# Layer 0 of a two-layer decoder trunk: another matmul form for the 16 recurrence projections, and another order of gates, outputs and heads

## The chip, the cores and the metric

The kernel runs on one core of a Trainium2 chip. The metric is device time in microseconds (us) of one execution; three runs of the kernel before gave a median of 2206.34 us (2206.28 to 2206.48). The engines that matter: TensorE (PE in the profile, its weight loads PEld), VectorE (DVE), ScalarE (ACT), and SyncE (SP), which issues the weight transfers. Each engine works through its own queue in the order in which the program was laid out, and waits on semaphores where an operand or a buffer is not ready.

## The reference, cut to what matters

The trunk has a batch of one, 256 tokens and a width of 2048. Layer 0 projects the normalised input into a recurrence (RG-LRU, 1024 wide, with a gated output) and into eight HGRN2 heads, and maps both through one output projection; a squared-ReLU MLP follows. Layer 1 is attention with an MLP. The change touches only layer 0's mixer:

```
proj = h @ w_in
x_lru, y_lru, q_h, f_h, v_h, g_h = jnp.split(proj, list(IN_SPLITS), axis=-1)
lru = rg_lru(causal_depthwise_conv(x_lru, conv_w, conv_b), w_a, b_a, w_i, b_i, lam)
lru = lru * jax.nn.gelu(y_lru.astype(F32), approximate=True)
hg = hgrn2(q_h, f_h, v_h, g_h, lower_bound, g_norm)
mixed = jnp.concatenate([lru, hg], axis=-1).astype(h.dtype)
return mixed @ w_out
```

Inside `rg_lru`, the two gates `r` and `i` are block-diagonal products (four blocks of 256) of the convolved `x_lru`, each through a sigmoid; `a` is an exponential of `r`, and a scan over the 256 tokens gives the recurrence.

## The kernel before

**Precision.** Every float32 matmul is made of three: each operand is split into a high part (rounded to fp32r) and a low part (the rest), and high·high, high·low and low·high are added in PSUM. Weights come in tiles of 128x2048; `Weights.split` makes `hi` (a ScalarE cast, line 104) and `lo` (a VectorE subtraction, line 105), in two halves of 128x1024 in this stage. `hi`, `lo` and `raw` have three buffers each, so a tile's split waits until the tile three before it is used up.

**Two forms of one projection.** A projection (`project`) makes a 128x256 block of features by tokens from 16 blocks of the input. The activations stand in `bufa` as 16 blocks of 512 columns: 256 of the high part, 256 of the low part. `direct` (lines 210 to 216) issues per block three matmuls of 256 columns (hi by high, hi by low, lo by high), all into the same 256 columns of PSUM. `cross` (lines 204 to 208) issues per block one matmul of 512 columns (hi by high and low at once, into two halves of a PSUM bank), and, after all 16 of them, 16 matmuls of 256 columns for lo by high. The halves of the bank must then be added: `scaled` (line 408) copies the second half to SBUF on ScalarE (line 414), adds the first half on VectorE (line 415) and multiplies by the norm's scale (line 416). After `direct`, one VectorE multiplication does (line 411). The MLP's up-projections use `cross`; `HA`, `XA` and `YA` (line 218) say which form the heads, the recurrence's inputs and its outputs use.

**The order.** `ORDER` (line 853) lists layer 0's steps; it also sets the order in which weights are fetched. `v` (two steps) makes the values of four heads: 4 weight tiles, matmuls of 512 columns into two PSUM banks, copied out by ScalarE (line 345) into `vg`. That pool has one buffer, so the second `v` can be copied out only when head 3 has used the first. `h` is a head: three projections (q, f, g) and between them a ladder of dependent steps: lines 471 (two small matmuls), 474 (a masked copy, VectorE) and 488 (a multiplication, VectorE), for group sizes 1 to 64, then lines 466 and 495 to 497 and a transpose (line 509). `x` is a recurrence input: one projection, then line 525 on ScalarE, three VectorE steps on line 527 (the convolution), and the split into `bufb` (lines 230 and 231). `g` makes the gates of four x blocks: one weight tile, eight PSUM tiles of six 256-column matmuls each, every one copied out by a ScalarE sigmoid; then tanh, exp and sqrt on ScalarE with table loads between, VectorE steps on lines 545 to 553 and a scan (line 554). `y` is an output: one projection, a GeLU made of a square, a sigmoid and VectorE steps on lines 562 to 565, and the split into `bufb`. `out_project` then multiplies `bufb` by the output weights, in groups 2, 3 (heads), 0, 1 (recurrence).

**What sets the order of the work.** Projection and gate matmuls go through `mm`, which chains them: on PE they stand in the order of the program text. The ladder's matmuls are not in the chain; the framework's scheduler puts them between. `lut` keeps ScalarE's table functions in program order, group by table. There are three PSUM banks for projections and gates (`pmm`); `pl` has two, `pd`, `po` and `pt` one each.

Of the kernel before, what the change touches and what calls it, by code (L numbers as in the profile page):

```python
# [40 lines left out]
def trunk_kernel(ctx, tc, x, xtok, cols, tab, masks, pos, fin, w_in, w_gate, w_out, w_qkv, w_o, w1, w2, out):  # L41
# [28 lines left out]
    def plan2(i, products):  # L70
# [3 lines left out]
        for what, u in PRODUCTS:  # L74
# [3 lines left out]
             "v": (w_in, lambda i: 16 + 16 * i, 4), "h": (w_in, lambda i: 20 + i // 4 * 16 + i % 4 * 3, 3)}  # L78
    for step in ORDER.split():
        src, first, n = where[step[0]]  # L80
# [134 lines left out]
            mm(p, h, mov[:, S:], start=False, stop=False)  # L215
            mm(p, l, mov[:, :S], start=False, stop=last)

    HA, XA, YA = direct, direct, direct

    def folded(p, name="z", bufs=None, home=None):  # L220
        with urgent():
# [346 lines left out]
    vgroups = {}  # L568
    for step in ORDER.split():
        i = int(step[1])  # L570
# [279 lines left out]

PRIO = 150
URGENT = 400
ORDER = "v0 h0 x0 h1 x1 h2 x2 h3 x3 v1 h4 x4 h5 x5 h6 x6 h7 x7 g0 y0 y1 y2 y3 g1 y4 y5 y6 y7"
WARM = 12
LINE = 64
PAIRS = 2
# [107 lines left out]
```

## Time and profile before

| | us |
|---|---|
| median of three runs | 2206.34 |
| profiled execution | 2206.14 |
| its span on the core | 2204.3 |
| PE busy | 2180.6 |
| DVE busy | 1673.1 |
| ACT busy | 1110.0 |

The span is the time from the first to the last instruction of the program in the profile; 1.8 us of the profiled execution lie outside of it. "Busy" for PE counts pipelined matmuls whose ends overlap, so that the price of one matmul is not its duration in a row but the distance from its start to the next one's start. A row of the timeline gives the start (us from the span's start), the time from the first start to the last end of the merged instructions, the engine, the line, the tiles and their shapes, and in brackets the idle time before it with what ended it. Layer 0's mixer takes about the first 336 us; then come the output projection, the MLP and layer 1.

### The profile page before, as it was taken

Reading aid. Unit: us, or ns where it says so; the run is one execution under the profiler, and the core shown is the slowest. Engines: PE = TensorE matmul, PEld = TensorE weight load, DVE = VectorE, ACT = ScalarE, POOL = GpSimd, SP = SyncE. Lnnn points to the kernel's source line nnn. Section 1 sums busy time; section 2 is a strip of 40 time slices with the busy share of each in tenths; the row PEclk is TensorE's granted clock in tenths of the full one; section 3 lists DMA queues with packets and bytes.
Section 4 is the critical chain, followed back from the end, with each engine's and each line's share of the span. In section 5 each row is a group of like instructions: output and inputs, shape, how many; then the busy total and the mean of one; then the engine's idle time right before and its main releaser. Section 6 shows DMA issues by size and latency. Waiting matters only on the chain.

```text
span 2204.3 us, 29702 instructions
## 1 busy us (share of the span) xinstructions
PE 2180.6 (99%) x12004; PEld 1897.7 (86%) x12004; DVE 1673.1 (76%) x2286; ACT 1110.0 (50%) x1364; POOL 15.8 (1%) x23
## 2 busy tenths in 40 slices
PE   9999999999999999999999999999999999999997
PEld 8999998888888888888888888888888888888886
DVE  8767796578878877877967868556797697687787
ACT  6444485545444444544654444454454454455454
POOL 0000000000000000000000000000000000000000
PEclk9999999999999999999999999999999999999999
DMA  8444446555655755755654554655566566566553
GB/s 313 156 168 156 153 154 232 181 198 191 232 199 181 248 194 172 248 208 165 217 195 169 174 188 157 227 191 179 165 214 246 174 205 248 191 191 248 191 191 115
DMA packets 61017, 431.25 MB, mean 196 GB/s; under 512 B 6784, under 2 KB 7552, under 8 KB 9424
## 3 DMA queue, kind: packets, MB, share of 16 engines
q1 hardware_dynamic: 58320, 412.20, 53.2%
q0 software_dynamic: 2560, 17.16, 4.3%
q8 instruction: 94, 1.54, 0.3%
q14 instruction: 43, 0.35, 0.0%
HBM read 427.48 MB, written 2.10 MB: 195 GB/s over the span
## 4 chain that ended last, share of the span: by engine, by line
PE 84%; DVE 9%; ACT 3%; DMA 2%; issue 1%; SPq 0%; ACTq 0%; DVEq 0%
PE p L176 75%; DVE lo L105 5%; PE po L176 5%; DVE a L142 2%; ACT hi L104 2%; DMA a<-in_w 2%; PE pd L176 1%; PE pl L471 1%; DVE xall L650 1%; PE pl L179 0%; PE pl L777 0%; DVE bufa L234 0%; PE po L798 0%; DMA xall<-in_x 0%; PE pd L790 0%
## 5 line engine op out<-in xcount | busy, mean ns | idle before, releaser
L105 DVE TENSOR_TENSOR lo<-raw,hi 128x1024 fp32r<-128x1024 f32 (+2 forms) x486 | 822.1, 1709 | 341.8 <-ACT hi L104 322.2
L104 ACT CAST hi<-raw 128x1024 fp32r<-128x1024 f32 (+2 forms) x486 | 688.2, 1441 | 663.3 <-PE p L176 515.3
L176 PE MATMUL p<-bufa,hi 128*128 128x512 f32 (+1 forms) x3840 | 854.5, 357 | 2.4 <-DVE bufa L234 2.4
L176 PEld LDWEIGHTS p<-bufa,hi 128*128 128x128 f32 x3840 | 672.0, 190 | 95.2 <-DVE bufa L234 3.8
L176 PE MATMUL p<-bufa,lo 128*128 128x256 f32 x3200 | 521.9, 285 | 0.0
L176 PEld LDWEIGHTS p<-bufa,lo 128*128 128x128 f32 x3200 | 452.6, 191 | 12.7
L176 PE MATMUL p<-hi,bufb 128*128 128x512 f32 x1408 | 451.9, 391 | 1.6 <-DVE xall L650 1.6
L176 PEld LDWEIGHTS p<-hi,bufb 128*128 128x128 f32 x1408 | 264.5, 188 | 59.1 <-DVE xall L650 5.0
L176 PE MATMUL p<-lo,bufb 128*128 128x512 f32 x704 | 275.3, 391 | 3.8 <-DVE lo L105 3.8
L104 ACT CAST hi<-a 128x2048 fp32r<-128x2048 f32 x64 | 122.4, 1913 | 161.7 <-PE p L176 81.1
L105 DVE TENSOR_TENSOR lo<-a,hi 128x2048 fp32r<-128x2048 f32 x64 | 146.5, 2289 | 58.4 <-ACT hi L104 58.4
L176 PEld LDWEIGHTS p<-lo,bufb 128*128 128x128 f32 x704 | 132.3, 188 | 33.7 <-DVE lo L105 7.2
L176 PE MATMUL p<-hi,bufa 128*128 128x512 f32 x384 | 123.6, 396 | 0.7 <-ACT hi L104 0.7
L176 PEld LDWEIGHTS p<-hi,bufa 128*128 128x128 f32 x384 | 72.3, 188 | 16.0 <-ACT hi L104 1.6
L176 PE MATMUL pd<-hi,bufb 128*128 128x512 f32 x256 | 84.3, 390 | 0.2 <-DVE xall L650 0.2
L176 PE MATMUL po<-hi,bufb 128*128 128x512 f32 x256 | 84.2, 390 | 0.3 <-DVE xall L650 0.3
L176 PE MATMUL p<-hi,forms 128*128 128x512 f32 x256 | 84.1, 389 | 0.0
L176 PE MATMUL p<-lo,bufa 128*128 128x512 f32 x192 | 76.3, 397 | 1.8 <-DVE lo L105 1.8
L142 DVE TENSOR_TENSOR a<-a,raw 128x2048 f32<-128x2048 f32 x32 | 73.1, 2283 | 0.0
L223 ACT COPY t<-p 128x256 f32<-128x256 f32 x128 | 46.7, 365 | 41.2 <-PE p L176 40.7
L650 DVE SCALAR_TENSOR_TENSOR xall<-p,nm,xall 128x512 f32<-128x512 f32 x64 | 47.7, 746 | 19.3 <-PE p L176 19.2
L230 ACT CAST bufb<-zp 128x256 fp32r<-128x256 f32 x128 | 50.4, 401 | 18.7 <-DVE zp L684 18.7
(239 smaller groups left out, 1803.6 us busy)
## 6 DMA issues: line engine op xcount, KB each, us to landing
raw<-in_w SPq DMA_DIRECT2D x224, 1024.0 KB, 4.8
raw<-in_w_qkv SPq DMA_DIRECT2D x48, 1024.0 KB, 4.8
raw<-in_w_in SPq DMA_DIRECT2D x46, 1024.0 KB, 4.8
raw<-in_w_out SPq DMA_DIRECT2D x16, 1024.0 KB, 4.8
a<-in_w SPq DMA_DIRECT2D x16, 1024.0 KB, 4.8
t<-in_w SPq DMA_DIRECT2D x16, 1024.0 KB, 5.0
t<-in_w POOLq DMA_DIRECT2D x16, 1024.0 KB, 8.0
raw<-in_w_o SPq DMA_DIRECT2D x16, 1024.0 KB, 4.8
```

Source lines behind the costliest of these rows:

```text
L104: A.copy(h, w)
L105: V.tensor_tensor(l, w, h.bitcast(F32), OP.subtract)
L142: V.tensor_tensor(r, r, held[add], OP.add)
L176: chain[:] = [after(T.matmul(*args, **kw), chain)]
L223: A.copy(t, p[:, S:])
L230: A.copy(dst[:, :S], src)
L471: T.matmul(pl[:, j], kq[:, js], halves(qp[:, js], c, True), start=True, stop=True)
L650: V.scalar_tensor_tensor(xres[:, j, at], bank, (r2 if sign > 0 else r2n)[:, j:j + 1], xres[:, j, at], op0=OP.mult, op1=OP.add)
```

## The change

Two lines change. The recurrence's input and output projections go from `direct` to `cross`, and the steps of `ORDER` are rearranged: `g0` (the gates of x blocks 0 to 3) now follows `v1`, the outputs `y0` to `y3` stand one behind each of the heads 4 to 7, and `g1` follows `x7` at once.

```diff
-    HA, XA, YA = direct, direct, direct
+    HA, XA, YA = direct, cross, cross
@@
-ORDER = "v0 h0 x0 h1 x1 h2 x2 h3 x3 v1 h4 x4 h5 x5 h6 x6 h7 x7 g0 y0 y1 y2 y3 g1 y4 y5 y6 y7"
+ORDER = "v0 h0 x0 h1 x1 h2 x2 h3 x3 v1 g0 h4 y0 x4 h5 y1 x5 h6 y2 x6 h7 y3 x7 g1 y4 y5 y6 y7"
```

The form that the 16 projections now use, and what follows it:

```python
def cross(p, w, jobs):
    for blk, mov, first, last in jobs:
        mm(p, w.part(blk * P, P)[0], mov, start=first, stop=False, skip_group_check=True)
    for blk, mov, first, last in jobs:
        mm(p[:, S:], w.part(blk * P, P)[1], mov[:, :S], start=False, stop=last, skip_group_check=True)

def scaled(p, z, acc=None):
...
            t = tmp.tile([P, S], F32, name="t1", bufs=2)
            A.copy(t, p[:, S:])
            V.tensor_tensor(z, p[:, :S], t, OP.add)
            V.tensor_tensor(z, z, rs, OP.mult)
```

The order of the weight transfers follows `ORDER`; their number and sizes stay.

## The prediction

> **What bounds the kernel now.** I read the page's head and its chain of waits first.
>
> ```profile
> span 2204.3 us, 29702 instructions
> PE 2180.6 (99%) x12004; PEld 1897.7 (86%) x12004; DVE 1673.1 (76%) x2286; ACT 1110.0 (50%) x1364; POOL 15.8 (1%) x23
> PE 84%; DVE 9%; ACT 3%; DMA 2%; issue 1%; SPq 0%; ACTq 0%; DVEq 0%
> ```
>
> TensorE fills the span; a stage gets shorter only when its matmuls take less or when PE waits less. The layer's stages by windows (length, then busy time of PE, PEld, DVE and ACT, POOL, granted clock, DMA share, GB/s):
>
> ```profile
> 50.00:164.50 114.50, 114.50 (x883) 110.49 (x882) 83.04 (x201) 49.76 (x89) 0.00 (x0) 1.00 0.48 162
> 164.50:272.10 107.60, 107.53 (x910) 107.34 (x909) 78.67 (x192) 48.45 (x93) 0.00 (x0) 1.00 0.46 157
> 272.10:335.85 63.75, 62.69 (x522) 62.17 (x521) 58.14 (x143) 53.01 (x102) 0.52 (x1) 1.00 0.45 157
> ```
>
> Heads and inputs (second row) leave DVE 27% free; gates and outputs (third) load DVE to 91% and ACT to 83%. The clock is 1.00 throughout and the DMA engines are half idle. PE's few real waits in the mixer, from its timeline:
>
> ```profile
> 170.53 0.39 PE L466 MATMUL pl<-qk 128*128 128x128 f32 x2
> 170.99 0.50 PE L176 MATMUL p<-bufa,hi 128*128 128x256 f32 x2
> ...
> 306.57 0.28 PE L176 MATMUL p<-bufb,lo 128*128 128x256 f32 x1
> 307.73 0.51 PE L176 MATMUL p<-bufb,hi 128*128 128x256 f32 x2 [0.88 <-DVE z L411]
> ...
> 308.43 0.28 PE L176 MATMUL p<-bufb,lo 128*128 128x256 f32 x1
> 308.89 0.50 PE L176 MATMUL p<-bufb,hi 128*128 128x256 f32 x2 [0.18 <-ACT gr L199]
> ```
>
> Start to start, less what the instruction itself takes: 1.04 and 0.34 at g1, 0.3 behind v1, together 1.7 us. So the change is worth its matmuls, plus at most 1.7, minus the new waits. From the output projection on, the changed program has the same PE order, so all of it happens in the mixer.
>
> **The matmuls of 16 projections.** One `direct` projection (y7, first and last row, then what follows it) and one `cross` projection (of the MLP):
>
> ```profile
> 330.09 0.40 PE L176 MATMUL p<-bufa,hi 128*128 128x256 f32 x2
> ...
> 335.73 0.28 PE L176 MATMUL p<-bufa,lo 128*128 128x256 f32 x1
> 335.85 0.40 PE L176 MATMUL p<-hi,bufb 128*128 128x512 f32 x1
> ```
>
> ```profile
> 433.76 3.81 PE L176 MATMUL p<-bufa,hi 128*128 128x512 f32 x16
> 437.41 2.08 PE L176 MATMUL p<-bufa,lo 128*128 128x256 f32 x16
> 439.32 3.82 PE L176 MATMUL p<-bufa,hi 128*128 128x512 f32 x16
> ```
>
> Direct: 335.85 - 330.09 = 5.76 us, 48 x 0.120. Cross: 439.32 - 433.76 = 5.56, 16 x 0.228 + 16 x 0.119. Saved 0.20 each, **-3.2 us** for 16.
>
> The Trainium skill ("TensorE: Matmul & The Clock Gate", section "Wait — 56ns, not 53.3ns?") prices a warm matmul at its columns over 2.4 GHz plus about 2.5 ns; since both forms stream the same 12,288 columns, its saving would be 16 x 2.5 ns = 0.04 us a projection, 0.6 us in all, which speaks against the change. The rows above disagree: 0.120 for 256 columns and 0.228 for 512 leave 12 ns per instruction, and I go by them.
>
> **The fold.** Each of the 16 gains a ScalarE copy and a VectorE addition:
>
> ```profile
> L223 ACT COPY t<-p 128x256 f32<-128x256 f32 x128 | 46.7, 365 | 41.2 <-PE p L176 40.7
> L225 DVE TENSOR_TENSOR zp<-p,t 128x256 f32<-128x256 f32 x16 | 6.7, 417 | 0.5 <-ACT t L223 0.5
> ```
>
> 16 x 0.365 = 5.8 us on ACT and 16 x 0.42 = 6.7 on DVE, off PE's path: a bank is refilled three tiles later. It lengthens the way from x7's last matmul to its gates, below. Were the cover gone, the 0.8 us would stand on the path.
>
> **The moved steps.** y0 to y3 among the heads bring DVE, per head round, two weight halves (2.4), seven operations of 0.42 and x's fold: 5.4 us. A round has now 27 us of PE and 19.8 of DVE (second window over four), then 32.5 and 25.2, 77%: covered. Weight transfers only change order. Four places are not covered.
>
> *1. g0 behind v1.* v1 holds two of the three banks until head 3 has used the first `vg`:
>
> ```profile
> L345 ACT ACTIVATE vg<-p,nr x2: 683/685/687, 175.6 to 176.2; 128x512 f32<-128x512 f32 x2
>   PE po L497: 2.7, 1
> ```
>
> v1's matmuls ended at 163.7, the copy began at 175.6, released by L497. Now head 4's q and f use the third bank; after the change the gates do, so six of them pass one bank, each waiting for the sigmoid of the one before:
>
> ```profile
> L199 ACT ACTIVATE gr<-p,c__82 128x256 f32<-128x256 f32 x8 | 3.8, 473 | 0.7 <-PE p L176 0.6
> L104 ACT CAST hi<-raw 128x1024 fp32r<-128x1024 f32 x130 | 129.9, 1046 | 70.6 <-issue 37.1 <-PE p L176 30.0 <-ACT st L479 1.5
> ```
>
> A gate is 6 x 0.12 = 0.72 of PE, and 0.53 passes until its bank is free: seven times 0.53 = 3.7 idle. Head 3's rungs fill about 3.0 of it. A rung costs PE 169.61 - 169.04 - 0.12 = 0.45:
>
> ```profile
> 169.04 0.55 PE L471 MATMUL pl<-qk 128*128 128x64 f32 x4
> 169.41 0.36 PE L176 MATMUL p<-bufa,lo 128*128 128x256 f32 x1
> 169.61 0.40 PE L176 MATMUL p<-bufa,hi 128*128 128x256 f32 x2
> ```
>
> On ACT, head 4's f weights (two halves, 2.0) stand ahead of the first sigmoid and need a buffer that v1's last matmul frees, which adds 1.1. **+1.8** (0.4, as now, to 4, nothing filled).
>
> *2. Head 4's ladder* starts behind g0's table functions. By ACT's order, counted from row durations, its second sigmoid ends 27.3 us after v1, and PE reaches the ladder's first product at 27.5. **+0.3** (0 to 2).
>
> *3. x7, then g1 at once.* The gates' matmuls are chained, and those of blocks 6 and 7 need x7's convolution. Now that stretch (first row x7's scaling, last its split) has g0 and y0 on PE behind it:
>
> ```profile
> 272.29 0.42 DVE L411 TENSOR_TENSOR xp<-p,nr 128x256 f32<-128x256 f32 x1 [0.54 <-PE p L176]
> ...
> 279.65 0.42 DVE L231 TENSOR_TENSOR bufb<-xc,bufb 128x256 fp32r<-128x256 f32 x1 [0.23 <-ACT bufb L230]
> ```
>
> It takes 7.8 us there. In the changed order 17 DVE instructions stand between x7's fold and its split (5.6 us at 0.20 to 0.40 start to start), the fold's turn comes 2.6 late behind a weight half for y5, and ScalarE steps (0.6 and 0.4) lie between: 8.6 us for the high part. Until then PE has 27 gate matmuls (3.2), five rungs (2.25) and a transpose (0.3), 5.8 in all. Three rungs of head 7 stand there with nothing between. **+2.8** (0 where the seven steps run with nothing between them, 0.37 + 2 x 0.42 + 0.6 + 3 x 0.48 + 2 x 0.41 = 4.1, under 5.8; 6 where the 7.8 stretches as before and the 2.6 and 1.1 come on top).
>
> *4. y6's bank.* The output projection's second PSUM tile takes y6's bank. Now y6 is scaled (336.35) before the next weight tile's halves; in the changed DVE order its fold stands behind both halves of that tile, which need y7's weight buffer:
>
> ```profile
> 336.35 0.42 DVE L411 TENSOR_TENSOR z<-p,nr 128x256 f32<-128x256 f32 x1
> 336.69 0.42 DVE L564 TENSOR_TENSOR z<-z,q 128x256 f32<-128x256 f32 x1
> 337.14 0.42 DVE L565 TENSOR_TENSOR z<-z,xc 128x256 f32<-128x256 f32 x1
> 337.48 2.35 DVE L105 TENSOR_TENSOR lo<-raw,hi 128x1024 fp32r<-128x1024 f32 x2
> ```
>
> From y7's last matmul: 2.3 (start to start) + 1.2 (four small steps) + 0.42 = 3.9; PE has 12 matmuls of 0.227 = 2.7. **+1.2** (0 to 4 where DVE comes late).
>
> For the ladder's other places I add **+0.5**, a little over the one such wait of now (0.3). **Sum**: -3.2 - 1.7 + 1.8 + 0.3 + 2.8 + 1.2 + 0.5 = +1.7. The profiled execution took 2206.14 (span 2204.3 and 1.8 around), 0.2 below the median: 2206.1 + 1.7 = **2207.8 us**. A difference of 0.2% (4.4 us) is about what a measurement of this kernel can tell from no change, so this is no change.
>
> **The rivals.**
>
> *Slower: DVE is late at x7.* If VectorE reaches x7's fold one weight tile (2.3) and two rungs (2 x 1.1) later than I counted, the gates wait 7.3 instead of 2.8, and DVE carries some 2 us of it to y6's bank: +6.5, **2214.3**. For it: 91% of DVE in the stage that g1 heads, and that in-order queues hand every delay on. Against: PE waited only 1.7 us there until now. It decides once x7's split ends over 11.5 us after x7's last matmul.
>
> *Faster: the waits are covered.* x7's steps at 4.1 us lie within PE's 5.8, y6's fold comes in time, g0 costs the 0.4 of now: -3.2 - 1.7 + 0.9 = -4.0, **2202.1**. For it: the shortest chain fits. Against: the order has 17 DVE instructions there, not seven.
>
> *Columns are all that counts.* If a 256-column matmul among 512s costs half of one (0.114), cross saves nothing against 48 x 0.114 and the sum is +4.9 from the waits: **2211.0**. That is the mechanism of the page of the Trainium skill named above. The 16 matmuls in 1.91 us of row 437.41 speak against it.
>
> **How the numbers follow.** Forecast 0.60, slower rival 0.30, faster 0.07, columns 0.03. Faster by over 0.2% needs nearly every wait gone (half of the 0.07, and a little of the forecast's tail): 0.06. Slower takes the slower rival, the columns and the forecast's tail: 0.35. The same: 0.59. The range reaches from 2202.5, the covered case, to 2214.5, the slower rival; the forecast's own is 2204 to 2211.
>
> **What would show it.** In the profile after: x and y projections as x16 and x16 rows 5.56 us apart; sigmoids of gates between single gates behind v1, and 1 to 3 us of PE idle there; a PE gap of 2 to 4 us before g1's second half, released by DVE bufb L231 or ACT bufb L230; a gap of about 1 us at the output projection's second tile, released by DVE L415. Wrong would be: no gap at g1; a gap over 6 us; or rungs waiting for DVE all through heads 4 to 7.

## The result and the profile after

| | before | after |
|---|---|---|
| median of five runs, us | 2206.34 (2206.06 to 2206.71) | 2215.43 (2214.9 to 2216.29) |
| profiled execution, us | 2206.14 | 2215.43 |
| its span, us | 2204.3 | 2213.6 |

The change makes the kernel 9.1 us slower, a ratio of 1.0041 (1.0031 to 1.0052). The spans differ by 9.3 us, so the trace holds all of it. The page's head and its chain of waits after:

```profile
span 2213.6 us, 29236 instructions
PE 2182.8 (99%) x11748; PEld 1886.1 (85%) x11748; DVE 1681.0 (76%) x2302; ACT 1115.5 (50%) x1380; POOL 15.8 (1%) x23
PE 84%; DVE 9%; ACT 3%; DMA 2%; issue 1%; SPq 0%; ACTq 0%; DVEq 0%
```

The shares of the page are those of before: they don't show a loss of 0.4%. It is 256 matmuls fewer (16 projections, 16 each), and yet more time. The stages by windows do show it (length, then busy time of PE, PEld, DVE, ACT and POOL, granted clock, DMA share, GB/s; the cuts are the ends of v1 and of x7 and the start of the output projection):

```profile
161.95:302.75 140.80, 139.03 (x1046) 132.66 (x1045) 110.43 (x265) 78.00 (x150) 0.00 (x0) 1.00 0.46 161
302.75:339.77 37.02, 34.05 (x211) 30.81 (x210) 29.83 (x76) 28.74 (x58) 0.52 (x1) 0.95 0.36 122
339.77:351.00 11.23, 7.73 (x28) 5.94 (x27) 9.85 (x24) 3.14 (x9) 0.00 (x0) 0.85 0.54 187
```

PE is idle for 1.8, 3.0 and 3.5 us in them, and in the second and third the clock is below 1.00, which it nowhere was in the windows of before. PE's waits up to 350 us (in total, times, longest), those that are new:

```profile
PE p L176 <- DVE z L415: 3.5, 1, 3.5
PE pl L471 <- DVE qk L488: 2.3, 3, 1.2
...
PE p L176 <- ACT gr L199: 1.1, 1, 1.1
...
PE p L176 <- ACT bufb L230: 0.7, 1, 0.7
```

To compare kernels I use one sum for a stretch, called its loss below: for every pair of neighbouring matmuls, the distance from start to start, less the median distance of pairs of the same two shapes in the kernel before, added up where it is over 0.06 us. It holds waits and lowered clock alike, and comes from the one profiled execution of each kernel. A rung below is one group size of a head's ladder (line 471 on PE, then 474 and 488 on VectorE).

**Behind v1** (g0 now stands there), PE's timeline:

```profile
162.88 0.55 PE L471 MATMUL pl<-qk 128*128 128x64 f32 x4
164.56 0.50 PE L176 MATMUL p<-bufb,hi 128*128 128x256 f32 x2 [1.13 <-ACT gr L199]
```

and what ScalarE did in that time:

```profile
162.15 1.99 ACT L104 CAST hi<-raw 128x1024 fp32r<-128x1024 f32 x2 [3.37 <-PE p L176]
164.05 0.47 ACT L199 ACTIVATE gr<-p,c__82 128x256 f32<-128x256 f32 x1
```

The first gate's sigmoid stands behind a weight tile's two casts, which waited 3.37 us for v1's last matmul. Four more gaps of 0.36 follow, each behind matmuls of the ladder or of the head's products. The loss from 160 to 180 us is 3.84, before 0.75.

**Between x7 and the outputs:**

```profile
302.75 0.28 PE L176 MATMUL p<-bufb,hi 128*128 128x256 f32 x1
...
307.65 0.63 PE L471 MATMUL pl<-qk 128*128 128x64 f32 x4 [0.35 <-DVE qk L488]
309.52 0.63 PE L471 MATMUL pl<-qk 128*128 128x64 f32 x4 [1.24 <-DVE qk L488]
310.83 0.66 PE L471 MATMUL pl<-qk 128*128 128x64 f32 x4 [0.68 <-DVE qk L488]
312.19 0.52 PE L176 MATMUL p<-bufb,hi 128*128 128x256 f32 x1 [0.70 <-ACT bufb L230]
...
313.92 0.63 PE L176 MATMUL p<-bufb,hi 128*128 128x256 f32 x2
314.35 0.41 PE L176 MATMUL p<-bufb,lo 128*128 128x256 f32 x1
314.56 0.63 PE L176 MATMUL p<-bufb,hi 128*128 128x256 f32 x2
```

Three rungs of head 7 wait for VectorE one after another, then the gates wait for x7's high part: 3.65 us by the loss's way of counting. Then three matmuls of 256 columns take 314.56 - 313.92 = 0.64 us where they took 0.36: PE runs at about half its speed until 315.8, and 1.7 us of the loss are this. The loss from 300 to 320 us is 5.71, before 1.67.

**At the output projection's second tile,** PE, then VectorE:

```profile
342.29 0.39 PE L176 MATMUL p<-hi,bufb 128*128 128x512 f32 x1
346.17 0.55 PE L176 MATMUL p<-hi,bufb 128*128 128x512 f32 x1 [3.50 <-DVE z L415]
346.52 0.63 PE L176 MATMUL p<-lo,bufb 128*128 128x512 f32 x1
346.95 1.05 PE L176 MATMUL p<-hi,bufb 128*128 128x512 f32 x2
```

```profile
342.14 1.21 DVE L105 TENSOR_TENSOR lo<-raw,hi 128x1024 fp32r<-128x1024 f32 x1
...
343.48 1.21 DVE L105 TENSOR_TENSOR lo<-raw,hi 128x1024 fp32r<-128x1024 f32 x1
344.61 0.41 DVE L562 SCALAR_TENSOR_TENSOR q<-q,z 128x256 f32<-128x256 f32 x1
344.95 0.41 DVE L231 TENSOR_TENSOR bufb<-z,bufb 128x256 fp32r<-128x256 f32 x1
345.28 0.41 DVE L745 TENSOR_TENSOR cosT<-cosT,sinT 32x256 f32<-32x256 f32 x1
345.62 0.41 DVE L415 TENSOR_TENSOR z<-p,t 128x256 f32<-128x256 f32 x1
```

The last row is y6's fold, which frees the bank. It comes right after y4's split (344.95), both behind the two weight halves. After the wait the granted clock is low:

```profile
346.17:349.59 3.42, 3.42 (x9) 2.65 (x10) 3.17 (x11) 1.13 (x3) 0.00 (x0) 0.54 0.66 266
350.00:360.00 10.00, 10.00 (x46) 8.26 (x45) 6.21 (x9) 7.23 (x11) 0.00 (x0) 1.00 0.49 170
```

The loss from 320 to 380 us is 5.50, before 0.26. The three differences, 3.09 + 4.04 + 5.24 = 12.4, less the 3.2 that the columns save, are 9.2 of the span's 9.3 us.

### The profile page after: what moved, and what is told of

Same layout as the page of the kernel before. It is cut to its first block, busy times and chain, and to the rows that moved or that the text cites. A ratio compares the mean times of both kernels' runs of the same rounds, so it can differ in the third digit from the quotient of the medians.

```text
span 2213.6 us, 29236 instructions
## 1 busy us (share of the span) xinstructions
PE 2182.8 (99%) x11748; PEld 1886.1 (85%) x11748; DVE 1681.0 (76%) x2302; ACT 1115.5 (50%) x1380; POOL 15.8 (1%) x23
## 4 chain that ended last, share of the span: by engine, by line
PE 84%; DVE 9%; ACT 3%; DMA 2%; issue 1%; SPq 0%; ACTq 0%; DVEq 0%
PE p L176 75%; DVE lo L105 5%; PE po L176 5%; DVE a L142 2%; ACT hi L104 2%; DMA a<-in_w 2%; PE pd L176 1%; PE pl L471 1%; DVE xall L650 1%; PE pl L179 0%; PE pl L777 0%; DVE bufa L234 0%; PE po L798 0%; PE pd L790 0%; DMA xall<-in_x 0%
## 5 line engine op out<-in xcount | busy, mean ns | idle before, releaser
L176 PE MATMUL p<-bufa,hi 128*128 128x512 f32 (+1 forms) x3584 | 823.1, 369 | 2.4 <-DVE bufa L234 2.4
L176 PEld LDWEIGHTS p<-bufa,hi 128*128 128x128 f32 x3584 | 638.3, 189 | 104.1 <-DVE bufa L234 3.8
L176 PE MATMUL p<-bufa,lo 128*128 128x256 f32 x3200 | 484.3, 284 | 0.0
L176 PEld LDWEIGHTS p<-bufa,lo 128*128 128x128 f32 x3200 | 436.7, 191 | 14.0
L230 ACT CAST bufb<-zp 128x256 fp32r<-128x256 f32 x128 | 50.3, 399 | 18.5 <-DVE zp L684 18.5
```

What stands on the lines that cost most here:

```text
L176: chain[:] = [after(T.matmul(*args, **kw), chain)]
L230: A.copy(dst[:, :S], src)
```

## The experiments

Twelve kernels ran, each beside the kernel before (2206.2 to 2206.3 in all of them). Medians, and the three losses:

| kernel | median, us | 160-180 | 300-320 | 320-380 |
|---|---|---|---|---|
| before | 2206.3 | 0.75 | 1.67 | 0.26 |
| after | 2215.43 | 3.84 | 5.71 | 5.50 |
| e1 fold everywhere, old order | 2211.03 | 1.28 | 2.23 | 7.48 |
| e2 no fold, new order | 2210.47 | 3.13 | 4.50 | 0.18 |
| e3 after, other bank | 2212.78 | 5.01 | 5.61 | 2.54 |
| e4 after, idle matmuls in the wait | 2214.58 | 3.84 | 6.92 | 0.86 |
| e5 fold on x, old order | 2204.86 | 1.28 | 1.90 | 0.26 |
| e6 fold on x and y0 to y3, old order | 2206.05 | 1.28 | 2.22 | 1.64 |
| e7 after, y3 behind x7 | 2216.35 | 3.84 | 0.44 | 12.41 |
| e8 after, g0 behind h4 | 2212.32 | 1.28 | 4.77 | 5.51 |
| e9 e1, y6 in its own tile | 2208.77 | 1.28 | 2.22 | 4.98 |
| e10 after, y6 in its own tile | 2211.17 | 3.84 | 6.45 | 0.17 |
| e11 no fold, g0 alone moved | 2207.02 | 3.14 | 0.55 | 0.26 |

(e12, told last, isn't comparable. e3 has after's PE order from 160 to 180 us; its 5.01 there against 3.84 is a low clock, 0.50 from 166.4 to 169.7, in that execution.)

### e1 and e2: the two halves of the change

```diff
e1, the kernel before with
-    HA, XA, YA = direct, direct, direct
+    HA, XA, YA = direct, cross, cross
e2, the kernel before with
-ORDER = "... v1 h4 x4 h5 x5 h6 x6 h7 x7 g0 y0 y1 y2 y3 g1 y4 y5 y6 y7"
+ORDER = "... v1 g0 h4 y0 x4 h5 y1 x5 h6 y2 x6 h7 y3 x7 g1 y4 y5 y6 y7"
```

> The order of before, with the 16 projections in the cross form. Theory (the columns save 0.20 us each, the fold is covered, and every loss of the change comes from its order): 2206.3 - 3.2 = 2203.1, between 2202 and 2205. Rival (the fold loads VectorE and ScalarE until PE waits for them): 2206 or more, with new PE waits released by DVE L415 or ACT L414.

> The new order, with the 16 projections in the direct form of before. Theory (the order's waits are the loss, whatever the form): 2206.3 + 9.1 + 3.2 = 2218.6 if the waits are the same, 2214 to 2219 since the shorter evacuation of x7 and y6 can take up to 3 us off the waits. Rival (the fold makes the waits): under 2209.

Measured: 2211.03 (ratio 1.0023, 1.0014 to 1.0031) and 2210.47 (1.0018, 1.0009 to 1.0028). My theory, that the fold is harmless and the order costs everything, fell, and e2's rival (under 2209) isn't met either: each half costs, 4.8 and 4.2 us, and their sum is 9.0 of the 9.1 of both. By place they don't add up so well: e1 loses 7.48 from 320 to 380 us and both together 5.50, e2 4.50 at g1 and both 5.71. In e1 the columns' gain is there (the output projection starts at 333.97, before 335.85) and is lost in one place, in PE's and then VectorE's timeline:

```profile
336.49 0.39 PE L176 MATMUL p<-hi,bufb 128*128 128x512 f32 x1
341.90 0.77 PE L176 MATMUL p<-hi,bufb 128*128 128x512 f32 x1 [5.02 <-DVE z L415]
```

```profile
336.68 2.32 DVE L105 TENSOR_TENSOR lo<-raw,hi 128x1024 fp32r<-128x1024 f32 x2
...
340.34 0.41 DVE L231 TENSOR_TENSOR bufb<-z,bufb 128x256 fp32r<-128x256 f32 x1
...
341.35 0.41 DVE L415 TENSOR_TENSOR z<-p,t 128x256 f32<-128x256 f32 x1
```

So the wait at the second tile is the fold's, not the order's (e2 has none), and the losses behind v1 and x7 are the order's.

### e3 and e4: what the second tile's 5.3 us are

```diff
e3, after, in out_project:
-        ps = [pmm.tile([P, 512], F32, name="p") for _ in range(2)]
+        ps = [pmm.tile([P, 512], F32, name="p") for _ in range(1 if src is w_out and i0 == 0 else 2)]
+        if len(ps) == 1:
+            ps.append(psc.tile([P, 512], F32, name="pd", bufs=1))
e4, after, between the first and the second tile's matmuls:
+                if src is w_out and i0 == 0 and g == kgs[0] and (j, i) == (0, 3):
+                    idle = psc.tile([P, P], F32, name="po", bufs=1)
+                    for _ in range(FILL):
+                        mm(idle, ones, ones, start=True, stop=True)
...
+FILL = 14
```

> The changed kernel, whose output projection puts its second PSUM tile of the first column block into the free bank pd in place of y6's bank. The rest of the order is the same. Theory (the wait for y6's fold and the slow matmuls behind it are the last 5.3 us of the loss): 2215.4 - 5.3 = 2210.1, no gap at the second tile and no lower clock there. Rival (VectorE is simply late and PE waits at the next thing that it makes): 2213 to 2215.4, with the gap at a weight tile or at bufb a little later.

> The changed kernel with 14 idle matmuls of 128 columns (some 3.1 us, into the free bank po) between the output projection's first and second tile, where PE waits 3.6 us for y6's bank. The wait stays. Theory (the idle time costs twice: once as a wait, and once because TensorE's clock is halved behind it): the second tile starts when it did, its matmuls are 0.227 apart and not 0.43, and the time is 2215.4 - 1.6 = 2213.8. Rival (the slow matmuls have another cause, such as the transfers that run then): 2215.4 or more, still 0.43 apart.

e3 gave 2212.78 (1.0032, 1.0021 to 1.0043), between the two: with a free bank the wait and the low clock at the second tile are gone, but PE then waits 1.24 and 0.91 us at 359 and 361 for y7's features. About half of the gain comes back, and the first of these waits is ScalarE's: VectorE has y7's product ready at 357.16 (L567 there), but the cast of its high part starts at 360.07, behind a table load, the cosine and sine for layer 1 and two casts of a weight tile. e4 gave 2214.58 (1.004, 1.0027 to 1.0054). PE, busy with the idle matmuls, is at full speed after them (line numbers are 4 higher in this kernel):

```profile
344.08 3.29 PE L176 MATMUL po<-ones 128*128 128x128 f32 x28
347.73 0.47 PE L176 MATMUL p<-hi,bufb 128*128 128x512 f32 x1 [0.36 <-DVE z L419]
348.03 0.39 PE L176 MATMUL p<-lo,bufb 128*128 128x512 f32 x1
348.26 0.63 PE L176 MATMUL p<-hi,bufb 128*128 128x512 f32 x2
```

512-column matmuls are 0.23 apart there, against 0.43 in the same place of after, while the DMA engines are as busy (0.74 from 347.73 to 351.00, 0.66 in after). So the low clock follows from the idle time and is worth 1.6 us. The time alone wouldn't show it: it lies between the two expectations and isn't clear of after's; in the profiled execution 1.2 us came on top between 300 and 320.

### e5 and e6: fold on fewer projections, in the old order

```diff
e5, the kernel before with
-    HA, XA, YA = direct, direct, direct
+    HA, XA, YA = direct, cross, direct
e6, e5 with, in lru_out, for both uses of YA
-YA
+cross if b < 4 else YA
```

> The kernel before with its own order, only the eight input projections x0 to x7 in the 512- and 256-column form with the fold; the output projections y stay in the form of before. My theory: the fold costs time only where it is y's and queues behind the weight halves of the output projection. Here there is none of that, so the columns alone act: 8 x 0.20 = 1.6 us less, 2204.7 (2204.0 to 2205.6), and no wait over 1 us at the output projection's second tile. Rival: the fold itself (a ScalarE copy and a VectorE add more for each projection) makes VectorE late wherever it stands, so x's fold costs as y's does: 2206.3 or more.

> The kernel before with its own order, x0 to x7 and y0 to y3 in the form with the fold, y4 to y7 without. My theory: 12 x 0.20 = 2.4 us less and no wait at the output projection's second tile, since y6 has no fold: 2203.9 (2203.2 to 2205.2), under both kernels. Rival: y0 to y3 stand as a block between g0 and g1, their folds make VectorE late there and the lateness is carried to the output projection: 2206.5 to 2209, with a wait for VectorE at the gates g1 or at the second tile.

e5: 2204.86 (2204.29 to 2205.59, ten runs), as my theory had it. Its ratio, 0.9994 (0.9985 to 1.0003), leaves open no change at all, though the slowest of its ten runs is below the fastest of the 24 of the kernel before (2205.70). e6: 2206.05 (0.9999, 0.9991 to 1.0008), between the two. It starts the output projection 0.1 us earlier than e5 (334.65 against 334.74), and y6, which has no fold here, still releases its bank late:

```profile
338.67 0.50 PE L176 MATMUL p<-hi,bufb 128*128 128x512 f32 x1 [1.11 <-DVE z L411]
```

So it is not y6's own fold that makes the wait here: the folds of y0 to y3 are all that e6 has beyond e5, and they were enough to make VectorE late.

### e7 and e8: covering the gates

```diff
after:  "... v1 g0 h4 y0 x4 h5 y1 x5 h6 y2 x6 h7 y3 x7 g1 y4 ..."
e7:     "... v1 g0 h4 y0 x4 h5 y1 x5 h6 y2 x6 h7 x7 y3 g1 y4 ..."
e8:     "... v1 h4 g0 x4 h5 y0 x5 h6 y1 x6 h7 y2 x7 y3 g1 y4 ..."
```

> The changed kernel with x7 and y3 exchanged in the order (h7 x7 y3 g1 in place of h7 y3 x7 g1), so that one output projection stands between x7 and the gates that read x7's features. My theory: the 14.5 us from x7's last matmul to y4's first hold about 5.3 us beyond the work (waits for head 7's ladder and x7's split, and the lower clock after them); y3's matmuls fill the first, so 4 to 5.3 us less than the changed kernel: 2210.1 to 2211.4. Rival: VectorE's queue is what is late there, it is not relieved by the exchange, and the wait stays at g1 or moves to the output projection: 2213 or more.

> The changed kernel with g0 one head later and each later step moved with it (v1 h4 g0 x4 h5 y0 x5 h6 y1 x6 h7 y2 x7 y3 g1 y4 to y7). My theory: g0 no longer runs straight after v1's casts, so its 3.1 us go as well as g1's 5.3 us; what stays of the change is 3.2 us less by the columns and 5.3 us at the output projection's second tile: 2208.4 (2207 to 2210). Rival: the ladder of head 4, which now has only the projection v1 and the gates to stand in, or vg of head 4, brings the time back: 2212 or more.

e7: 2216.35 (1.0045, 1.003 to 1.006); the rival's number. The waits at g1 are gone, the output projection starts at 334.37, 5.4 us earlier than in after, and all of it is waited for again there, at head 7's transposes (L509). PE, and the stretch behind the start of the output projection by windows:

```profile
332.60 0.39 PE L497 MATMUL po<-vg,st 128*128 128x128 f32 x2
...
349.07 0.73 PE L509 MATMUL pt<-tab__179,ho 128*128 128x128 f32 x2 [7.03 <-ACT ho L506]
```

```profile
334.37:353.00 18.63, 9.75 (x40) 7.53 (x39) 16.39 (x51) 11.03 (x25) 0.00 (x0) 0.82 0.50 171
```

PE has 9.75 us of work there and VectorE 16.39 of 18.63. But the way from head 7's last products (L497) through its norm to the transposes is as long as in after: 16.5 us here, 16.4 there (316.36 to 332.80). It starts 16 us later, because the scheduler put two rungs of head 7 and what follows them behind g1, among y4 to y7 (314.51, 320.38, L466 at 326.38); in after they stand ahead of the last gates, where PE waits for them. So y3 didn't cover the ladder at g1: the ladder moved, and the wait with it.

e8: 2212.32 (1.0027, 1.0016 to 1.0037), the rival's number by another way. Place 1's loss went as I expected (1.28 left) and head 4's ladder took nothing back; but the loss at g1 stayed (4.77), as did the second tile's. The ladder of head 7 stands here as in after: its last rungs (306.24, 307.89) come ahead of the last gates, and PE waits for them. In e7 they had moved behind.

### e9 and e10: y6's tile

The order on VectorE was the same in each kernel that waited: y4's split, then y6's write of `z`. `z` has two buffers, so y6 may not be written before y4 is done. One edit, in e1 and in after:

```diff
-        y = tmp.tile([P, S], F32, name="z")
+        y = wk.tile([P, S], F32, name="hz", bufs=4) if b == 6 else tmp.tile([P, S], F32, name="z")
```

> The kernel with before's order and the fold on all 16 projections (2211.0), with one edit: y6's tile z is taken from another pool (hz, four buffers, idle by then), where before y6 must take the buffer that y4 has until its split. My theory: the bank's release at the output projection's second tile is late because y6's fold may not write z before y4's split, and on VectorE both stand behind two weight halves. With a tile of its own the fold stands ahead of them: the 5.2 us wait and the 2.1 us of lower clock after it go, and up to half of that comes back as later waits for VectorE: 2204.0 to 2207.5. Rival: VectorE has too much work in this stretch wherever the fold stands, and the wait only moves: 2209.5 or more.

> The changed kernel (2215.4) with the same single edit: y6's tile z from the other pool. My theory: the wait at the second tile (3.7 us) and the lower clock after it (1.6 us) go, and about half of it comes back at the later tiles that read y4 to y7, as it did with another bank: 2211 to 2213.3. Rival: the lateness is VectorE's whole queue since g1, and all of it comes back: 2214.5 or more.

In e9 the fold moves ahead of the halves, and the wait of 5.02 us is gone from the second tile. VectorE, then PE:

```profile
335.06 0.40 DVE L415 TENSOR_TENSOR hz<-p,t 128x256 f32<-128x256 f32 x1
...
336.99 2.32 DVE L105 TENSOR_TENSOR lo<-raw,hi 128x1024 fp32r<-128x1024 f32 x2
```

```profile
352.12 0.39 PE L176 MATMUL p<-hi,bufb 128*128 128x512 f32 x1
354.65 0.50 PE L176 MATMUL p<-hi,bufb 128*128 128x512 f32 x1 [2.14 <-ACT bufb L230]
...
356.13 1.22 PE L176 MATMUL p<-hi,bufb 128*128 128x512 f32 x2 [0.75 <-DVE bufb L231]
```

But 2208.77 (1.0012, 1.0003 to 1.0021) is 2.3 us less, not the 5 that my theory had at the middle, and lies between the two expectations: 16 us after the second tile PE waits for y7's features, low clock included 4.8 us. e10 gave 2211.17 (1.0021, 1.0012 to 1.0031), 4.3 us less than after. That is in my range, but not for my reason: there the wait goes and nothing comes back, while the loss at g1 is 0.7 larger. What differs between the two is the place of one cast on ScalarE. y7's product on VectorE and its cast in e9, then the cast in e10:

```profile
350.87 0.43 DVE L565 TENSOR_TENSOR z<-z,xc 128x256 f32<-128x256 f32 x1
...
352.32 1.97 ACT L104 CAST hi<-raw 128x1024 fp32r<-128x1024 f32 x2
354.20 0.40 ACT L230 CAST bufb<-z 128x256 fp32r<-128x256 f32 x1
```

```profile
358.20 0.41 ACT L230 CAST bufb<-z 128x256 fp32r<-128x256 f32 x1 [0.74 <-DVE z L565]
358.51 1.99 ACT L104 CAST hi<-raw 128x1024 fp32r<-128x1024 f32 x2
```

VectorE has the product ready 17.3 us after the output projection's start in e9 (333.96 to 351.30) and 17.6 in e10 (340.62 to 358.17), so it isn't earlier in e10. In e9 the cast then stands for 2.9 us behind a table load, the cosine and sine for layer 1 and a weight tile's casts; in e10 it stands ahead of those casts and runs at once. So `z`'s buffer made the wait at the second tile, and ScalarE's order sets what comes back. This last is read off the two traces; no run moves the cast alone.

### e11: g0 alone

```diff
the kernel before with
-ORDER = "... v1 h4 x4 h5 x5 h6 x6 h7 x7 g0 y0 y1 y2 y3 g1 y4 y5 y6 y7"
+ORDER = "... v1 g0 h4 x4 h5 x5 h6 x6 h7 x7 y0 y1 y2 y3 g1 y4 y5 y6 y7"
```

> The kernel before with no fold anywhere, and of the new order only g0's place: straight after v1, ahead of head 4; y0 to y3 stay between x7 and g1. My theory: place 1 costs what its waits show, 3.1 us less the 0.5 us that the kernel before loses there, and place 3 nothing since y0 to y3 cover x7's split and head 7's ladder: 2208.9 (2208.0 to 2209.8). Rival: g0's gates, gone from between x7 and y0, relieve VectorE and ScalarE there by as much: 2206 to 2207.

2207.02 (1.0005, 0.9995 to 1.0015), a hair above the rival's range and not clear of no change. Both are right in part: the loss behind v1 is 2.4 us more, as place 1 has it, and 1.1 us come back at x7, where g0 had waited. Of the order's 4.2 us, g0's place is then 0.7, which the runs can't tell from nothing, and the way of y0 to y3 among the heads, which leaves x7 and g1 side by side, the other 3.5.

### e12: a failed try

```diff
e5 with
-ORDER = "... h7 x7 g0 y0 y1 y2 y3 g1 ..."
+ORDER = "... h7 x7 y0 g0 y1 y2 y3 g1 ..."
```

> The kernel before with the fold on x0 to x7 alone, and one exchange in its order: y0 ahead of g0 (x7 y0 g0 y1 y2 y3 g1). With the fold on x alone 2204.9 were measured, and 1.9 us beyond the work remained around g0, of which 1.4 was one wait for head 7's ladder straight after x7. My theory: y0's 32 matmuls cover that ladder: 1.0 to 1.9 us less, 2203.0 to 2204.0. Rival: as with y3 between x7 and g1, what PE gains is waited for again at the output projection, since VectorE and the gates that follow are not earlier: 2204.7 or more.

2213.56 (1.0035, 1.0022 to 1.0049). In this order y0 multiplies block 0's features before the gates and the scan have changed them, and g0 reads for x0 what y0 wrote; so block 0 is not computed as in the reference, and g0 has to wait for the whole of y0. Its 7 us say nothing of the cover that I meant to try (by y0's 48 matmuls, not 32: y has the form of before in it).

## Why the prediction was wrong

The forecast was no change, 2207.8; the kernel is 0.41% slower, and 2215.43 lies above the range.

- **The matmuls of 16 projections: right.** y4 starts at 317.29 and y5 at 322.86, 5.57 apart, against 5.76 before. e5, which keeps the order of before, saved 1.4 us for eight. The rule of the Trainium skill ("TensorE: Matmul & The Clock Gate", section "Wait — 56ns, not 53.3ns?") would make an estimate of 8 x 0.04 = 0.3 us of it. The rows disagree with that; e5's time speaks against it too, but its interval doesn't exclude 0.3.
- **The fold, "off PE's path: a bank is refilled three tiles later": the step that failed.** e1 has the fold alone and loses 4.8 us, with the 3.2 saved. The fold's 0.8 us are covered for a bank in the middle of a projection; what I didn't cost is that they lengthen a chain through `z`'s two buffers in the stage that I had shown with VectorE at 91%. Each tile of y there waits for the one two before it. Without the fold (e2) the loss from 320 to 380 us is 0.18; with the fold but y6 in a tile of its own (e9) the wait at the second tile is gone.
- **Place 4: right place and releaser, too small by 4.0 us** (1.2 forecast, 5.2 measured). I let the two halves start when y7's last matmul ends; VectorE came to them 2.4 us later (342.14 against 339.77), so that the wait is 3.66. That was within my bound of 4. The 1.6 us of low clock after it were in no bound. I had put the fold's place behind the halves down to the weights; e9 shows that it is y4's hold on `z`.
- **Place 3: right mechanism, too small by 2.6** (2.8 forecast, less the 1.4 at g1 that before already lost; 4.0 more measured). PE resumes 9.4 us after x7's last matmul (312.19 - 302.75), with 5.8 us of work in it, just as counted; the chain is 9.4 instead of 8.6. (The parts that I gave, 5.6, 2.6, 0.6 and 0.4, make 9.2 end to end; 8.6 takes one ScalarE step as covered.) Most of the 3.65 us end with VectorE's rungs, not with x7's split, so the rows that I named (L231 or L230) end only 0.89 of it. Of the remaining 2 us 1.7 are low clock, again not priced.
- **Place 1: right mechanism, too small by 1.6** (1.8 less 0.3; 3.1 measured). The wait for the casts is 1.32 (1.1 forecast), but the ladder's matmuls don't fill a gate's gap: 0.36 remain in each of four.
- **Place 2 and the ladder elsewhere: not seen.** 0.8 too much.
- **The sum:** 4.0 + 2.6 + 1.6 - 0.8 = 7.4 of the 7.6 us between 2207.8 and 2215.43. Low clock, for which the prediction had no term, is 1.6 + 1.7 = 3.3 of it.
- **The rivals.** The slower one has nearly the measured time (2214.3), but not by its own condition: x7's split ends 9.85 us after x7's last matmul (312.17 + 0.43), not over 11.5. Its reason, that in-order queues hand each delay on, is seen at the second tile, where y4's split and y6's fold stand behind two weight halves, and on ScalarE in e3 and e9.

A version under both kernels is e5, the fold on the inputs alone: 2204.86 against 2206.3, with an interval that reaches no change.

## What to carry to other kernels

In a stage where a second engine is as busy as VectorE here (91% before), an instruction added "off the path" has to be followed through the buffers that its result and its source hold, not only priced by its cover: here two buffers of a small tile decided when a PSUM bank came free. A wait that is removed can come back at the next consumer: about half of it did in e3, two thirds in e9, all in e7 and nothing in e10. Follow what that consumer needs (here one cast on ScalarE, in e7 the moved ladder) before counting the gain. And a wait of several microseconds on TensorE cost here the wait plus the slower matmuls after it: 3.66 and 1.6 us in after, 5.18 and 2.1 in e1.

## What the runs showed of the hardware that I had not expected

After a wait of 3.66 us the granted clock was 0.54 over the next 3.4 us, in e1 after 5.18 us it was 0.50:

```profile
341.90:345.45 3.55, 3.55 (x9) 2.81 (x10) 3.31 (x11) 1.75 (x5) 0.00 (x0) 0.50 0.33 138
```

In e1 it fell during the wait: it was 1.00 from 336.04 to 339.45 and 0.50 from 339.46 to 346.27, and at the fall PE had been idle for some 2.6 us. In after it was still 1.00 from 343.00 to 346.40 and 0.50 from 346.42 to 349.82, so it fell just after PE had resumed (346.17).

It also dropped at g1 after four waits of 0.5 to 1.4 us with matmuls between them, none of them long. How much it cost there changed from kernel to kernel with the same PE order in that stretch: the loss from 300 to 320 us was 5.71, 5.61, 6.92 and 6.45 in after, e3, e4 and e10.

The Trainium skill ("TensorE: Matmul & The Clock Gate", section "Part 1: The HAM clock gate") says that the clock falls to half after an idle window of some 3.4 us and returns after a busy one, and that the window runs freely. The rows agree with the half, with the length (3.4 us in after, twice that in e1), and with a fall that comes at another point of the wait in each kernel. They don't agree with a whole window of idle time: some 2.6 us were enough in e1. That several short waits bring it down, none of them a whole idle window, is what its section "A second HAM failure mode: psum-queue depth-cycling" tells of another kernel; the stretch after x7 shows it here.
